# VectorE makes 7 tokens and one single product, ScalarE three products, in the second output tile of each group from the second on

## The chip, the cores and the metric

The kernel runs on one core of a Trainium2 chip. A core has engines with instruction streams of their own: PE (TensorE, matrix products), DVE (VectorE, elementwise work on whole tiles), ACT (ScalarE, elementwise work with one scalar for each partition), POOL (GpSimd) and SP (SyncE, which here only issues transfers). They work on SBUF, an on-chip memory of 128 partitions. Transfers between SBUF and the large HBM memory run on 16 DMA engines, which all queues share. A transfer is issued by an engine's queue and signals a semaphore when it has landed.

The metric is the time of one execution on the device in microseconds (us). The time before is a median of 240.11 us over 3 runs.

## The reference

Every token's row of 512 numbers is written twice, once times each of the token's two expert weights:

```python
batch, seq, hidden, n_experts = 16, 1024, 512, 8
k = 2
x_expanded = x[:, :, np.newaxis, :].repeat(k, axis=2)
weights = expert_weights[..., np.newaxis]
return (x_expanded * weights).astype(np.float32)
```

`x` has 16,384 tokens, all in float32. The indices of the experts are not used. The input is 33.6 MB, the output twice that.

## The kernel before

The tokens are cut into seven groups of 19, 19, 18, 18, 18, 18 and 18 tokens for each of the 128 partitions (`groups`, line 30). In a group every partition holds consecutive tokens, so its share of a group is one contiguous piece of HBM. A group is loaded into an `x_tile` (two buffers) and written in two output tiles, `o_tile` (three buffers), its two "halves": 10 and 9 tokens for the first two groups, 9 and 9 for the others. An output tile of 9 tokens has 9 x 2 x 512 numbers a partition, 36,864 bytes.

The weights come in first by two small transfers. PE transposes them twice so that `w_tile` has, for each partition, the two weights of each of its tokens as columns (`weights_columns`, `weights_out`). This is over after the first group.

The loop at line 161 runs over the groups, and inside it over the two halves. For a half, `products` (line 134) makes the output tile, and SP issues its transfer to HBM (line 170). After both halves, `load(i + 2)` (line 176) has ScalarE's queue issue the load of the group after next into the buffer that has just been used up (line 128). The first group's load is cut in two; groups 0 and 1 are loaded ahead of the loop.

`products` splits a half of `n` tokens between two engines. VectorE makes the first `m` tokens, both weights of each, in one `tensor_tensor` (line 136), in which `x_tile` is repeated for the two weights and `w_tile` over the 512 numbers. ScalarE makes the rest, one `mul` for each token and weight (line 149), each 512 numbers a partition with the weight as the scalar of the partition. `m` is all of the tokens in the very first half and `n - 1` afterwards, so that ScalarE has two products in each half but the first.

The order of instructions on each engine is the order in which the program is written (`manual_schedule`, line 110). Semaphores add the waits: a product waits for its `x_tile` to be loaded and for its `o_tile` to be free, that is, for the output transfer that last read it; a transfer of the output waits for both engines' products; a load waits until both engines have read the old group. On ScalarE's queue a load therefore stands between the products of one group and those of the next.

Of the kernel before, what the change touches and what calls it, by code (L numbers as in the profile page):

```python
# [1 line left out]

# [4 lines left out]


@with_exitstack
def kernel(  # L10
    ctx: ExitStack,
    tc: tile.TileContext,
    x: bass.AP,
    expert_indices: bass.AP,
    expert_weights: bass.AP,
    out: bass.AP,
):
    nc = tc.nc

    batch, seq, hidden = x.shape  # L20
    k = expert_weights.shape[-1]
    P = nc.NUM_PARTITIONS
    ntok = batch * seq
    assert ntok % P == 0

    f32 = mybir.dt.float32
    row = k * hidden


    groups = [19, 19, 18, 18, 18, 18, 18]  # L30
    assert sum(groups) * P == ntok
    TX = max(groups)
    TO = (TX + 1) // 2

    xf = x.rearrange("b s h -> (b s) h")
    of = out.rearrange("b s k h -> (b s) (k h)")
    wf = expert_weights.rearrange("b s k -> (b s) k")

    w_pool = ctx.enter_context(tc.tile_pool(name="w_pool", bufs=1))
    x_pool = ctx.enter_context(tc.tile_pool(name="x_pool", bufs=2))  # L40
    o_pool = ctx.enter_context(tc.tile_pool(name="o_pool", bufs=3))

    raw_pool = ctx.enter_context(tc.tile_pool(name="raw_pool", bufs=1))
    psum = ctx.enter_context(
        tc.tile_pool(name="psum", bufs=2, space=bass.MemoryType.PSUM)
    )

    w_tile = w_pool.tile([P, sum(groups) * k], f32)

    def rows(flat, done, T):  # L50
        return flat[done * P : (done + T) * P, :].rearrange("(p a) n -> p (a n)", a=T)

    B = 8
    M = P // B
    ident = w_pool.tile([P, P], f32)
    nc.gpsimd.memset(ident, 0.0)  # L59
    nc.gpsimd.affine_select(  # L60
        out=ident,
        in_=ident,
        compare_op=mybir.AluOpType.not_equal,
        fill=1.0,
        base=0,
        pattern=[[-1, P]],
        channel_multiplier=1,
    )

    def weights_in(eng, head, G, T):  # L70
        raw_tile = raw_pool.tile([G * M, B * T * k], f32, name=f"raw{T}_tile")
        eng.dma_start(
            out=raw_tile,
            in_=wf[head * P : (head + G * T) * P, :].rearrange(
                "(q a) n -> q (a n)", a=B * T
            ),
        )
        return raw_tile

    def weights_columns(raw_tile, G, T):  # L80
        n = T * k
        col_tile = raw_pool.tile([n, G * P], f32, name=f"col{T}_tile")
        cols = col_tile.rearrange("c (q r) -> c q r", r=B)
        for r0 in range(0, B, B // 2):
            up_tile = psum.tile([n, B // 2, G * M], f32)
            for r in range(B // 2):
                nc.tensor.transpose(  # L87
                    up_tile[:, r, :],
                    raw_tile[:, (r0 + r) * n : (r0 + r + 1) * n],
                    ident[: G * M, : G * M],  # L90
                )
            nc.vector.tensor_copy(  # L92
                out=cols[:, :, r0 : r0 + B // 2],
                in_=up_tile.rearrange("c r q -> c q r"),
            )
        down_tile = psum.tile([P, G * n], f32)
        for g in range(G):
            nc.tensor.transpose(  # L98
                down_tile[:, g * n : (g + 1) * n],
                col_tile[:, g * P : (g + 1) * P],  # L100
                ident[:n, :n],
            )
        return down_tile

    def weights_out(down_tile, head, G, T):
        nc.vector.tensor_copy(  # L106
            out=w_tile[:, head * k : (head + G * T) * k], in_=down_tile
        )

    ctx.enter_context(tc.manual_schedule())  # L110

    starts = [sum(groups[:i]) for i in range(len(groups))]
    loaded = []


    def halves(i):
        T = groups[i]
        return [T - T // 2, T // 2]

    def load(i):  # L120
        if i >= len(groups):
            return
        x_tile = x_pool.tile([P, TX * hidden], f32)
        loaded.append(x_tile)
        src = rows(xf, starts[i], groups[i])
        lo = 0
        for n in halves(i) if i == 0 else [groups[i]]:
            nc.scalar.dma_start(
                out=x_tile[:, lo * hidden : (lo + n) * hidden],
                in_=src[:, lo * hidden : (lo + n) * hidden],  # L130
            )
            lo += n

    def products(o_tile, x_tile, at, n, w_at):
        m = n - 1 if w_at else n
        nc.vector.tensor_tensor(  # L136
            out=o_tile[:, : m * row].rearrange("p (t k h) -> p t k h", t=m, k=k),
            in0=x_tile[:, at * hidden : (at + m) * hidden]
            .rearrange("p (t h) -> p t h", t=m)
            .unsqueeze(2)  # L140
            .to_broadcast([P, m, k, hidden]),
            in1=w_tile[:, w_at : w_at + m * k]
            .rearrange("p (t k) -> p t k", t=m)
            .unsqueeze(3)
            .to_broadcast([P, m, k, hidden]),
            op=mybir.AluOpType.mult,
        )
        for c in range(m * k, n * k):
            nc.scalar.mul(  # L149
                out=o_tile[:, c * hidden : (c + 1) * hidden],  # L150
                in_=x_tile[:, (at + c // k) * hidden : (at + c // k + 1) * hidden],
                mul=w_tile[:, w_at + c : w_at + c + 1],
            )

    raw_a = weights_in(nc.sync, starts[0], 2, 19)
    load(0)
    raw_b = weights_in(nc.scalar, starts[2], 5, 18)
    load(1)
    weights_out(weights_columns(raw_a, 2, 19), starts[0], 2, 19)

    for i, T in enumerate(groups):
        x_tile = loaded[i]
        outr = rows(of, starts[i], T)
        at = 0
        for j, n in enumerate(halves(i)):
            if i == 0 and j == 1:
                down_b = weights_columns(raw_b, 5, 18)
            o_tile = o_pool.tile([P, TO * row], f32)
            products(o_tile, x_tile, at, n, (starts[i] + at) * k)
            nc.sync.dma_start(  # L170
                out=outr[:, at * row : (at + n) * row], in_=o_tile[:, : n * row]
            )
            at += n
        if i == 0:
            weights_out(down_b, starts[2], 5, 18)
        load(i + 2)

# [1 line left out]
_INS = ['x', 'expert_indices', 'expert_weights']  # L179
_OUTS = [((16, 1024, 2, 512), 'float32')]  # L180


# [23 lines left out]
```

## Time and profile before

| what | value |
|---|---|
| median of 3 runs | 240.11 us (239.59 to 240.15) |
| the profiled execution | 240.3 us |
| its span (first to last instruction) | 238.3 us |
| granted clock | 1.00 |
| VectorE products (line 136) | 14, 124.9 us busy |
| ScalarE products (line 149) | 26, 17.3 us busy |
| output transfers (line 170) | 14: two of 5120 KB, twelve of 4608 KB |
| loads of x (line 128) | 8 |
| HBM read and written | 33.69 MB and 67.11 MB |

The page of a profile gives each engine's busy time as a share of the span. It then gives the DMA queues, with the time that their packets took as a share of what 16 engines have in the span, and the chain of work that ended last, followed back from the last instruction. Instructions are grouped by source line, with the tile written and the tiles read, and their size as partitions x elements. Behind the bar stand the busy time and the mean duration in ns, then the engine's idle time just before them and what ended it. A transfer is listed with its size and the time from its issue to its landing. Windows give the same figures for a chosen stretch of time; a DMA packet is counted in the window in which it begins, so a short window can show a share above 1.

### The profile page before, as it was taken

The numbers are of one execution on the slowest core, as the hardware profiler recorded it, in microseconds if no ns is written. First come the engines' busy times: TensorE is split into PE (matmuls) and PEld (weight loads), VectorE is DVE, ScalarE is ACT, GpSimd is POOL, SyncE is SP. The second block draws the span as 40 slices with busy tenths as digits, with TensorE's granted clock in tenths as the row PEclk, the third lists the DMA queues.
The fourth block names the chain that finished last, engine by engine and source line by source line (L and its number), as shares of the span: only waits on it lengthen the run. The fifth ranks groups of instructions, "written<-read, shape, count | busy, mean of one in ns | idle before, by whom it ended". The sixth has DMA issues, their size and how long they took to land.

```text
span 238.3 us, 213 instructions
## 1 busy us (share of the span) xinstructions
PE 3.0 (1%) x23; PEld 2.3 (1%) x23; DVE 126.6 (53%) x20; ACT 18.6 (8%) x27; POOL 0.7 (0%) x6
## 2 busy tenths in 40 slices
PE   1021000000000000000000000000000000000000
PEld 1011000000000000000000000000000000000000
DVE  1499987391095077950494900778504949680000
ACT  0040020200020020200202000202002020200000
POOL 1000000000000000000000000000000000000000
DMA  7999899999999999999999999999999999999995
GB/s 275 426 465 425 352 443 473 404 402 483 404 424 418 439 483 402 421 470 402 446 439 402 483 402 421 439 427 446 415 433 458 421 433 433 427 446 415 433 458 235
DMA packets 3312, 100.80 MB, mean 423 GB/s; under 512 B 384, under 2 KB 496, under 8 KB 496
## 3 DMA queue, kind: packets, MB, share of 16 engines
q1 hardware_dynamic: 2064, 67.15, 65.4%
q10 hardware_dynamic: 1248, 33.65, 33.3%
HBM read 33.69 MB, written 67.11 MB: 423 GB/s over the span
## 4 chain that ended last, share of the span: by engine, by line
DMA 66%; DVE 23%; issue 0%; DVEq 0%; SPq 0%
DMA out_dram<-o_tile 62%; DVE o_tile L136 23%; DMA x_tile<-in_x_dram 4%; DVE col_tile L92 0%; DVEq L136 0%; SPq L170 0%
## 5 line engine op out<-in xcount | busy, mean ns | idle before, releaser
L136 DVE TENSOR_TENSOR o_tile<-x_tile,w_tile 128x8192 f32<-128x8192 f32 (+2 forms) x14 | 124.9, 8920 | 82.5 <-DMA out_dram<-o_tile 77.6
L149 ACT ACTIVATE o_tile<-x_tile,w_tile 128x512 f32<-128x512 f32 x26 | 17.3, 714 | 172.4 <-DMA out_dram<-o_tile 159.6
L92 DVE COPY col_tile<-up_tile 38x128 f32<-38x128 f32 (+1 forms) x4 | 1.4, 378 | 4.0 <-PE up_tile L87 4.0
L149 ACT ACT_TABLE_LOAD x1 | 1.3, 1283 | 15.3 <-DMA x_tile<-in_x_dram 15.3
L87 PE MATMUL up_tile<-ident,raw_tile 32*38 32x32 f32 (+1 forms) x16 | 1.8, 284 | 14.3 <-DMA raw_tile<-in_expert_weights_dram 14.3
L87 PEld LDWEIGHTS up_tile<-ident,raw_tile 32*38 32x38 f32 (+1 forms) x16 | 1.4, 135 | 14.4 <-issue 14.4
L98 PE MATMUL down_tile<-ident,col_tile 36*128 36x36 f32 (+1 forms) x7 | 1.2, 305 | 4.7 <-DVE col_tile L92 4.7
L98 PEld LDWEIGHTS down_tile<-ident,col_tile 36*128 36x128 f32 (+1 forms) x7 | 0.9, 209 | 5.1 <-DVE col_tile L92 5.1
L106 DVE COPY w_tile<-down_tile 128x76 f32<-128x76 f32 (+1 forms) x2 | 0.6, 284 | 0.5 <-PE down_tile L98 0.5
L60 POOL TENSOR_SCALAR_AFFINE_SELECT ident<-ident 128x128 f32<-128x128 f32 x1 | 0.3, 292 | 0.1
L59 POOL MEMSET ident<- 128x128 f32 x1 | 0.2, 204 | 0.3 <-POOLq L190 0.3
L190 POOL MEMSET const-bfloat16-1.0<- 128x1 bf16 x1 | 0.1, 101 | 0.0
L190 POOL MEMSET const-uint8-127<- 128x1 uint8 x1 | 0.1, 101 | 0.0
L190 POOL MEMSET const-float32-0.0<- 128x1 f32 x1 | 0.1, 98 | 0.2 <-issue 0.2
L190 POOL MEMSET const-float32-1.0<- 128x1 f32 x1 | 0.1, 98 | 0.0
## 6 DMA issues: line engine op xcount, KB each, us to landing
out_dram<-o_tile SPq DMA_DIRECT2D x12, 4608.0 KB, 35.4
x_tile<-in_x_dram ACTq DMA_DIRECT2D x5, 4608.0 KB, 26.6
out_dram<-o_tile SPq DMA_DIRECT2D x2, 5120.0 KB, 34.8
x_tile<-in_x_dram ACTq DMA_DIRECT2D x1, 4864.0 KB, 27.5
x_tile<-in_x_dram ACTq DMA_DIRECT2D x1, 2560.0 KB, 8.7
x_tile<-in_x_dram ACTq DMA_DIRECT2D x1, 2304.0 KB, 14.0
raw_tile<-in_expert_weights_dram ACTq DMA_DIRECT2D x1, 90.0 KB, 13.9
raw_tile<-in_expert_weights_dram SPq DMA_DIRECT2D x1, 38.0 KB, 2.7
```

Of the source, the lines that this page charges most:

```text
L59: nc.gpsimd.memset(ident, 0.0)
L60: nc.gpsimd.affine_select(out=ident, in_=ident, compare_op=mybir.AluOpType.not_equal, fill=1.0, base=0, pattern=[[-1, P]], channel_multipl ...
L87: nc.tensor.transpose(up_tile[:, r, :], raw_tile[:, (r0 + r) * n : (r0 + r + 1) * n], ident[: G * M, : G * M],)
L92: nc.vector.tensor_copy(out=cols[:, :, r0 : r0 + B // 2], in_=up_tile.rearrange("c r q -> c q r"),)
L98: nc.tensor.transpose(down_tile[:, g * n : (g + 1) * n], col_tile[:, g * P : (g + 1) * P], ident[:n, :n],)
L106: nc.vector.tensor_copy(out=w_tile[:, head * k : (head + G * T) * k], in_=down_tile)
L136: nc.vector.tensor_tensor(out=o_tile[:, : m * row].rearrange("p (t k h) -> p t k h", t=m, k=k), in0=x_tile[:, at * hidden : (at + m) * hidden]
L149: nc.scalar.mul(out=o_tile[:, c * hidden : (c + 1) * hidden], in_=x_tile[:, (at + c // k) * hidden : (at + c // k + 1) * hidden], mul=w_ti ...
L190: nc = _bacc.Bacc("TRN2", target_bir_lowering=False, num_devices=1)
```

## The change

From the second group on, the second half of a group is split in another way. VectorE's large product covers 7 of the 9 tokens in place of 8. VectorE then makes one more product itself, of a single token and weight, as a `tensor_scalar` with the weight as scalar. ScalarE makes the remaining three of these single products in place of two. The first halves, and both halves of the first group, stay as they were. Six output tiles are concerned.

```diff
-    def products(o_tile, x_tile, at, n, w_at):
-        m = n - 1 if w_at else n
+
+    def products(o_tile, x_tile, at, n, w_at, m, s):
         nc.vector.tensor_tensor(
             out=o_tile[:, : m * row].rearrange("p (t k h) -> p t k h", t=m, k=k),
             in0=x_tile[:, at * hidden : (at + m) * hidden]
...
             op=mybir.AluOpType.mult,
         )
         for c in range(m * k, n * k):
-            nc.scalar.mul(
-                out=o_tile[:, c * hidden : (c + 1) * hidden],
-                in_=x_tile[:, (at + c // k) * hidden : (at + c // k + 1) * hidden],
-                mul=w_tile[:, w_at + c : w_at + c + 1],
-            )
+            out = o_tile[:, c * hidden : (c + 1) * hidden]
+            x_in = x_tile[:, (at + c // k) * hidden : (at + c // k + 1) * hidden]
+            w = w_tile[:, w_at + c : w_at + c + 1]
+            if c < m * k + s:
+                nc.vector.tensor_scalar(
+                    out=out, in0=x_in, scalar1=w, scalar2=None, op0=mybir.AluOpType.mult
+                )
+            else:
+                nc.scalar.mul(out=out, in_=x_in, mul=w)
...
             o_tile = o_pool.tile([P, TO * row], f32)
-            products(o_tile, x_tile, at, n, (starts[i] + at) * k)
+
+            m, s = (n - 2, 1) if i and j else (n - 1, 0) if i or j else (n, 0)
+            products(o_tile, x_tile, at, n, (starts[i] + at) * k, m, s)
```

## The prediction

> **What bounds the kernel now.** I read the page first: the shares of the engines, then the DMA queues, then the chain that ended last.
>
> ```profile
> span 238.3 us, 213 instructions
> PE 3.0 (1%) x23; PEld 2.3 (1%) x23; DVE 126.6 (53%) x20; ACT 18.6 (8%) x27; POOL 0.7 (0%) x6
> DMA packets 3312, 100.80 MB, mean 423 GB/s; under 512 B 384, under 2 KB 496, under 8 KB 496
> q1 hardware_dynamic: 2064, 67.15, 65.4%
> q10 hardware_dynamic: 1248, 33.65, 33.3%
> DMA 66%; DVE 23%; issue 0%; DVEq 0%; SPq 0%
> ```
>
> VectorE (DVE) is busy half of the time and ScalarE (ACT) a twelfth. The two DMA queues, q1 for the outputs and q10 for the loads, together take 65.4 + 33.3 = 98.7% of what 16 DMA engines have in the span. The last line, the chain, gives VectorE 23%, which invites the thought that a shorter product shortens the kernel. So the second view is the DMA by stretches of time. The columns are the stretch, its length, the busy time of PE, PEld, DVE, ACT and POOL, the clock, the DMA share and GB/s.
>
> ```profile
> 20.00:234.00 214.00, 0.75 (x5) 0.61 (x5) 115.38 (x17) 16.01 (x24) 0.00 (x0) 1.00 1.00 432
> 200.00:234.00 34.00, 0.00 (x0) 0.00 (x0) 11.43 (x2) 1.33 (x2) 0.00 (x0) 1.00 1.00 434
> 235.00:236.00 1.00, 0.00 (x0) 0.00 (x0) 0.00 (x0) 0.00 (x0) 0.00 (x0) 1.00 0.51 221
> 236.00:237.00 1.00, 0.00 (x0) 0.00 (x0) 0.00 (x0) 0.00 (x0) 0.00 (x0) 1.00 0.01 0
> ```
>
> From 20 to 234 us the share is 1.00 at 432 GB/s, and it stays 1.00 at 434 GB/s after 200 us, when only outputs are left. A share of 1.00 means that all 16 engines always have a packet. All 100.80 MB at 432 GB/s take 233.3 us; the other 5.0 us of the span are the start, before there is anything to move, and the end. The change moves not a byte more or less.
>
> The third view asks how long a finished tile waits in the queue: the transfers of the output, over the whole span (first fence) and from 195 us on (second).
>
> ```profile
> L170 SPq DMA_DIRECT2D out_dram<-o_tile x14: 332/332/357, 20.4 to 213.7; - x14
> DMA to landing us min/median/max: 23.8/35.4/45.8
> ```
>
> ```profile
> L170 SPq DMA_DIRECT2D out_dram<-o_tile x2: 332/332/332, 202.8 to 213.7; - x2
> out_dram<-o_tile SPq DMA_DIRECT2D x2, 4608.0 KB, 23.8
> DMA to landing us min/median/max: 23.8/23.8/23.8
> ```
>
> A tile of 9 tokens is 4608 KB = 4.72 MB, at 434 GB/s 10.9 us of all engines. Yet no output lands sooner than 23.8 us after its issue. The last two were issued at 202.8 and 213.7 and landed at 226.6 and 237.5: exactly one transfer apart. The last tile was therefore handed over 226.6 - 213.7 = 12.9 us before the engines finished the one ahead of it. A transfer that found nothing ahead of it would still need its start-up. The smallest one in the trace bounds that:
>
> ```profile
> raw_tile<-in_expert_weights_dram SPq DMA_DIRECT2D x1, 38.0 KB, 2.7
> ```
>
> So the last changed tile could be 12.9 - 2.7 = 10.2 us later before an engine ran dry. The end of the kernel is set by bytes through the engines, and VectorE has a **cover of 10.2 us** there.
>
> The six products that the change touches are the second of each pair from 45 us on:
>
> ```profile
> 45.60 8.69 DVE L136 TENSOR_TENSOR o_tile<-x_tile,w_tile 128x8192 f32<-128x8192 f32 x1 [5.24 <-DMA out_dram<-o_tile]
> 84.95 8.69 DVE L136 TENSOR_TENSOR o_tile<-x_tile,w_tile 128x8192 f32<-128x8192 f32 x1 [10.22 <-DMA out_dram<-o_tile]
> 116.23 8.69 DVE L136 TENSOR_TENSOR o_tile<-x_tile,w_tile 128x8192 f32<-128x8192 f32 x1 [11.71 <-DMA out_dram<-o_tile]
> 150.50 8.69 DVE L136 TENSOR_TENSOR o_tile<-x_tile,w_tile 128x8192 f32<-128x8192 f32 x1 [13.30 <-DMA out_dram<-o_tile]
> 181.77 8.69 DVE L136 TENSOR_TENSOR o_tile<-x_tile,w_tile 128x8192 f32<-128x8192 f32 x1 [11.62 <-DMA out_dram<-o_tile]
> 204.93 8.69 DVE L136 TENSOR_TENSOR o_tile<-x_tile,w_tile 128x8192 f32<-128x8192 f32 x1 [2.19 <-DMA out_dram<-o_tile]
> ```
>
> In each the bracket says that VectorE stood idle before it until an earlier output had left the buffer that the product writes. With three buffers, one has then just landed and two are still in the queue: up to two transfers of 10.9 us against a product of 8.7 us, which gives 13.1 us, close to the 12.9 read above. VectorE waits for the DMA and not the other way round.
>
> **The change part by part.** *VectorE.* The product has three sizes in the trace, and there is a copy of two sizes as well:
>
> ```profile
> L136 DVE TENSOR_TENSOR o_tile<-x_tile,w_tile 128x8192 f32<-128x8192 f32 x12 | 104.3, 8692 | 77.6 <-DMA out_dram<-o_tile 77.6
> L136 DVE TENSOR_TENSOR o_tile<-x_tile,w_tile 128x10240 f32<-128x10240 f32 x1 | 10.8, 10826 | 4.3 <-DMA x_tile<-in_x_dram 4.3
> L92 DVE COPY col_tile<-up_tile 36x320 f32<-36x320 f32 x2 | 0.9, 474 | 0.0
> L106 DVE COPY w_tile<-down_tile 128x180 f32<-128x180 f32 x1 | 0.3, 329 | 0.0
> ```
>
> (10826 - 8692) / 2048 = 1.042 ns an element, and 8692 - 8192 x 1.042 = 156 ns fixed. Seven tokens, 7168 elements, come to 7.63 us, which is 1.07 less. The single product of 512 elements by one scalar a partition has no row. Nothing in the trace streams faster than 1.04 ns an element; for a lower bound I halve that, 156 + 512 x 0.52 = 0.42 us. Its upper bound is a second fixed part and two cycles an element, 156 x 2 + 512 x 2.08 = 1.38 us. The nearest rows are the copies, also with one input tensor: (474 - 329) / 140 = 1.04 ns an element, so 474 + 192 x 1.04 = 0.67 us. I take 0.67. A changed tile then needs 7.63 + 0.67 = 8.30 us against 8.69, so it is handed over 0.39 us earlier; by the bounds, 0.64 earlier to 0.32 later.
>
> The Trainium skill ("VectorE: DVE Perf Modes", The perf-mode tier table) lets an fp32 product with a scalar run at 2x from SBUF, while an fp32 product of two tensors stays at 1x. By that rule the estimate is the lower bound, about 0.43 us, and 0.63 us earlier; no row here has such an operation, and the time of the kernel would be the same.
>
> *ScalarE.* It gets a third product of this kind:
>
> ```profile
> L149 ACT ACTIVATE o_tile<-x_tile,w_tile 128x512 f32<-128x512 f32 x26 | 17.3, 714 | 172.4 <-DMA out_dram<-o_tile 159.6 <-DMA x_tile<-in_x_dram 12.7
> 204.92 1.33 ACT L149 ACTIVATE o_tile<-x_tile,w_tile 128x512 f32<-128x512 f32 x2 [9.57 <-DMA out_dram<-o_tile]
> ```
>
> 17.3 / 26 = 0.67 us each, so three take 2.0 us in place of 1.33. They start with VectorE's (204.92 beside 204.93) and end 6.3 us before its 8.30 are over, so they cost nothing; if ScalarE ran after VectorE and not beside it, the tile would be 8.30 + 2.0 = 10.3 us, 1.6 later than now and still inside the 10.2 of cover.
>
> *What is queued behind.* The load of the group after next is issued by ScalarE's queue once both engines have finished the second tile; the output is issued by SP's. Both move with the tile, 0.39 us earlier, and neither queue gets a DMA more.
>
> ```profile
> 124.99 0.33 SPq L170 DMA_DIRECT2D out_dram<-o_tile  x1
> 125.02 0.36 ACTq L128 DMA_DIRECT2D x_tile<-in_x_dram  x1
> DVE o_tile L136 <- DMA out_dram<-o_tile: 77.6, 11, 13.3
> DVE o_tile L136 <- DMA x_tile<-in_x_dram: 4.9, 2, 4.3
> ```
>
> VectorE waits for a load only twice, 4.9 us in all, 4.3 of it before the very first product (10240 elements); an earlier load is hidden. The 0.39 us go into the wait for a buffer, which is 77.6 us in 11 waits: VectorE idles that much longer, and each finished tile lies that much longer in the queue.
>
> *Sum.* The profiled execution took 240.3 us, with a span of 238.3. VectorE -6 x 0.39 = -2.3 us, all of it off the path; ScalarE +6 x 0.67 = +4.0 us, off the path; DMA bytes 0; path 0. That leaves 240.3. The median of the runs is 240.11, 0.19 below the profiled one, and I set the forecast on it: **240.1 us**.
>
> What can still move is the end. In the last two windows the engines do not stop together: 221 GB/s is 0.22 MB, six packets of 36,864 bytes (one partition's 9 tokens), begun after 235 us, while the other ten engines begin none. One packet on one engine takes 36,864 B / (432 / 16 GB/s) = 1.37 us. How the engines end up staggered may shift by half a packet either way, 0.7 us. That and the spread of the runs, 239.59 to 240.15, make the forecast's own range 239.4 to 240.8.
>
> **The rivals.** *Faster, by the chain taken at its word.* Two of the VectorE products in the chain belong to changed tiles:
>
> ```profile
> 116.23 8.71 DVE o_tile L136
> 124.99 36.28 DMA out_dram<-o_tile
> 204.93 8.69 DVE o_tile L136
> ```
>
> If each link shortened the end, 2 x 0.39 = 0.8 us would be gained, 2 x 0.64 = 1.3 by the lower bound: 239.3 down to 238.8 us on the median. Against it stands the link between them: a transfer worth 10.9 us of all engines takes 36.28 from issue to landing, so the chain runs through a queue that has other work to do, and that queue never empties (share 1.00).
>
> *Slower, because the single product stops the transfers.* The new operation may read SBUF at double rate through both ports and hold up the DMA engines that read the output tiles there. The place is the six single products; the price is at most their whole time, 6 x 0.67 = 4.0 us, or 6 x 0.42 = 2.5: 242.6 to 244.1 us. It decides from 0.72 / 6 = 0.12 us of stand-still at each. For it speaks only that no such operation is in the trace. Against it: with VectorE busy for 115.38 of 214 us the share is 1.00, and between products it is no better:
>
> ```profile
> 204.90:213.60 8.70, 0.00 (x0) 0.00 (x0) 8.67 (x1) 1.33 (x2) 0.00 (x0) 1.00 0.97 419
> 213.70:234.00 20.30, 0.00 (x0) 0.00 (x0) 0.00 (x0) 0.00 (x0) 0.00 (x0) 1.00 0.99 429
> ```
>
> 419 against 429 GB/s is a few packets counted on one side of an edge. The Trainium skill ("SBUF — State Buffer", Who interferes with whom) says that a VectorE operation in a two-port mode shuts out GpSimd, and so only the DMAs whose descriptors GpSimd writes. By that rule these transfers, of the kind hardware_dynamic on both queues, lose nothing and this rival falls; no run here shows it yet.
>
> *Slower, because a changed tile comes too late* (the pair of VectorE instructions costs far more than its rows, or a wait between the engines is added). Its price is only what exceeds the 10.2 us of cover, at the last tile; even the serial order above costs 1.6 of it. *That the change does not do what it says*, the product still of eight tokens, gives the same 240.1.
>
> **How the numbers follow.** A measurement of this kernel tells about 0.3%, 0.72 us, from no change. No change, with the range 239.4 to 240.8: 0.88. The chain at its word, 0.04, and a gain at the staggered end, 0.01, make faster 0.05. Stopped transfers 0.05 and a late tile or something unseen 0.02 make slower 0.07. The forecast's own range already leaves only 0.12 outside, so it stays the range.
>
> **What would show it.** Right: products of 7168 elements of 7.6 us, six single products of 0.4 to 0.7 us on VectorE, 32 ScalarE products in place of 26, VectorE's wait for output buffers longer by about 2 us than 77.6, the share still 1.00 at 432 GB/s from 20 to 234 us, the last two outputs still landing 10.9 us apart. The cover is wrong if the DMA share of any long stretch falls below 1.00, or if the shortest time to landing falls towards 10.9 us. The chain reading is right if the last output lands about 0.8 us sooner after the start although the GB/s stay the same; the port reading is right if the GB/s dip at the six single products.

## The result and the profile after

| | before | after |
|---|---|---|
| median of 15 runs | 239.68 us | 241.56 us |
| lowest and highest | 239.41, 242.02 | 239.52, 242.72 |
| runs above 240.6 us | 2 of 15 | 12 of 15 |
| the profiled execution | 240.3 us | 239.52 us |
| its span | 238.3 us | 237.6 us |

The changed kernel is **slower**: the ratio of the times is 1.0058, 95% interval 1.003 to 1.0085, against a forecast of no change. Both kernels reach 239.5 us, but the changed one seldom does; most of its executions take 241 to 242.7. The profiled execution happened to be the fastest of its 15, so this profile can't show the loss by itself. A later profile of the same kernel, its third, is of an execution of 241.25 us, and the two are shown side by side. In this document the ratios leave out executions more than 1.5% above the fastest of the same kernel (five in all), while medians, ranges and counts are over all executions.

First the page of the profiled execution, in the lines that answer to those of before:

```profile
span 237.6 us, 225 instructions
PE 3.0 (1%) x23; PEld 2.3 (1%) x23; DVE 122.6 (52%) x26; ACT 22.3 (9%) x33; POOL 0.7 (0%) x6
q1 hardware_dynamic: 2064, 67.15, 65.6%
q10 hardware_dynamic: 1248, 33.65, 33.3%
```

VectorE has 4.0 us less to do and ScalarE 3.7 more; the queues carry the same bytes. The groups of instructions, shapes kept apart, and the wait of VectorE for output buffers, in the same execution:

```profile
L136 DVE TENSOR_TENSOR o_tile<-x_tile,w_tile 128x7168 f32<-128x7168 f32 x6 | 45.7, 7625 | 54.9 <-DMA out_dram<-o_tile 54.9
L157 ACT ACTIVATE o_tile<-x_tile,w_tile 128x512 f32<-128x512 f32 x32 | 21.0, 713 | 168.6 <-DMA out_dram<-o_tile 155.9 <-DMA x_tile<-in_x_dram 12.6
L153 DVE TENSOR_SCALAR o_tile<-x_tile,w_tile 128x512 f32<-128x512 f32 x6 | 2.9, 480 | 0.0
```

```profile
DVE o_tile L136 <- DMA out_dram<-o_tile: 80.3, 11, 13.0
```

The reader sees the split as it was meant: a product of 7168 elements in 7.63 us, a single product in 0.48, and a wait for buffers that has grown from 77.6 to 80.3 us. One changed tile in order of time:

```profile
115.60 1.95 ACT L157 ACTIVATE o_tile<-x_tile,w_tile 128x512 f32<-128x512 f32 x3 [18.96 <-DMA out_dram<-o_tile]
115.69 7.62 DVE L136 TENSOR_TENSOR o_tile<-x_tile,w_tile 128x7168 f32<-128x7168 f32 x1 [11.66 <-DMA out_dram<-o_tile]
123.24 0.48 DVE L153 TENSOR_SCALAR o_tile<-x_tile,w_tile 128x512 f32<-128x512 f32 x1
123.78 0.33 SPq L176 DMA_DIRECT2D out_dram<-o_tile  x1
123.80 0.36 ACTq L128 DMA_DIRECT2D x_tile<-in_x_dram  x1
```

From the start of VectorE's product to the issue of the output it is 123.78 - 115.69 = 8.09 us; before it was 124.99 - 116.23 = 8.76. The tile is handed over 0.67 us earlier. I call this time, start of the product to issue of the output, the **hand-over time** below.

Now the end of the kernel. The windows have the columns of the prediction's; first the profiled execution, then the third profile, of 241.25 us:

```profile
20.00:234.00 214.00, 0.75 (x5) 0.61 (x5) 111.35 (x23) 19.69 (x30) 0.00 (x0) 1.00 1.00 433
235.00:236.00 1.00, 0.00 (x0) 0.00 (x0) 0.00 (x0) 0.00 (x0) 0.00 (x0) 1.00 0.09 37
236.00:237.00 1.00, 0.00 (x0) 0.00 (x0) 0.00 (x0) 0.00 (x0) 0.00 (x0) 1.00 0.01 0
```

```profile
20.00:234.00 214.00, 0.74 (x5) 0.60 (x5) 111.44 (x23) 19.69 (x30) 0.00 (x0) 1.00 1.00 432
235.00:236.00 1.00, 0.00 (x0) 0.00 (x0) 0.00 (x0) 0.00 (x0) 0.00 (x0) 1.00 0.34 147
236.00:237.00 1.00, 0.00 (x0) 0.00 (x0) 0.00 (x0) 0.00 (x0) 0.00 (x0) 1.00 0.26 111
```

From 20 to 234 us the two executions, 1.73 us apart in time, show the same share and 433 against 432 GB/s. The difference stands in the last row. One packet of 36,864 bytes begun in a window of 1 us counts 37 GB/s. In the first table a single packet begins after 235 us and none after 236; in the second, three packets (111 GB/s) begin after 236. They are the last packets of three DMA engines that run 1.8 us behind the other thirteen.

The trace has every DMA packet with its queue, start, duration and size, though not its engine. On a busy engine a packet begins 3 or 4 ns before the one ahead of it ends, so the packets string together into 16 sequences, one for each engine. This assignment is an inference, and after a pause on an engine it rests on which packet no other sequence explains. From them come the ends of the last output tile on the engines (us from the first instruction):

| profile | time | median engine ends | last engine ends | time - last end |
|---|---|---|---|---|
| before | 240.3 | 236.24 | 237.13 | 3.2 |
| before, second profile | 240.46 | 236.25 | 237.30 | 3.2 |
| after | 239.52 | 236.11 | 236.38 | 3.1 |
| after, second profile | 241.03 | 236.23 | 238.00 | 3.0 |
| after, third profile | 241.25 | 236.17 | 237.99 | 3.3 |

The median engine ends within 0.14 us of the same moment in all five. The time follows the last engine. Here is one of the thirteen engines and one of the late three in the third profile of after (start of the packet in us; o output, L load, s the small packet that signals the end of a transfer; the duration in ns where it isn't 1364; in brackets idle ns between packets):

```
on time  159.79:s  159.80:o  161.16:o        162.52:L        163.88:o        165.24:L        166.60:o
late     160.79:s  160.80:o  162.16:o 1929   (218) 164.30:L 1491  165.79:o   167.15:L
```

Both have packets of two queues to alternate between from 162 us on, when the load issued at 158.69 arrives. The late engine, 1.0 us behind at this point, takes 1929 ns for an output packet in place of 1364, then stands still for 218 ns and takes 1491 ns for its first load packet, and falls 0.91 us further behind. The other two late engines do much the same here. All three had lost about 0.4 us each before that, on the last packets of an earlier load (115.5 to 115.7 us: 1736 to 1766 ns), and nothing to speak of anywhere else after the start. In the other execution, of 241.03 us, two engines lost 1.5 and 1.1 us in the same two places, at 115.4 and 162.0 to 164.5 us.

### The profile page after: what moved, and what is told of

The parts are those of the page before. It is cut to its first block, busy times and chain, and to the rows that moved or that the text cites. A ratio compares the mean times of both kernels' runs of the same rounds, so it can differ in the third digit from the quotient of the medians.

```text
span 237.6 us, 225 instructions
## 1 busy us (share of the span) xinstructions
PE 3.0 (1%) x23; PEld 2.3 (1%) x23; DVE 122.6 (52%) x26; ACT 22.3 (9%) x33; POOL 0.7 (0%) x6
## 4 chain that ended last, share of the span: by engine, by line
DMA 66%; DVE 21%; issue 2%; DVEq 0%; SPq 0%
DMA out_dram<-o_tile 62%; DVE o_tile L136 20%; DMA x_tile<-in_x_dram 4%; DVE col_tile L92 0%; DVE o_tile L153 0%; DVEq L207 0%; DVEq L136 0%; SPq L176 0%
## 5 line engine op out<-in xcount | busy, mean ns | idle before, releaser
L136 DVE TENSOR_TENSOR o_tile<-x_tile,w_tile 128x8192 f32<-128x8192 f32 (+3 forms) x14 | 118.5, 8462 | 85.2 <-DMA out_dram<-o_tile 80.3
L157 ACT ACTIVATE o_tile<-x_tile,w_tile 128x512 f32<-128x512 f32 x32 | 21.0, 713 | 168.6 <-DMA out_dram<-o_tile 155.9
L153 DVE TENSOR_SCALAR o_tile<-x_tile,w_tile 128x512 f32<-128x512 f32 x6 | 2.9, 480 | 0.0
```

The costliest lines, as they stand in the source:

```text
L136: nc.vector.tensor_tensor(out=o_tile[:, : m * row].rearrange("p (t k h) -> p t k h", t=m, k=k), in0=x_tile[:, at * hidden : (at + m) * hidden]
L153: nc.vector.tensor_scalar(out=out, in0=x_in, scalar1=w, scalar2=None, op0=mybir.AluOpType.mult)
L157: nc.scalar.mul(out=out, in_=x_in, mul=w)
```

## The experiments

The runs have 10 to 15 timed executions, those without the loop's loads 4 and 5, and two runs were made for a profile alone. Each ratio is to the kernel before, timed in the same session on the same chip. The four kernels under "The remainder" were on a second chip and the two without loads on a third; the experiments ahead of them, with the changed kernel again, were all on one. The summary table stands at the end of this section.

**The changed kernel again**, no edit.

> The changed kernel as it is. Theory P (the split in itself moves the end): about 241.5 us, 1.8 above the kernel before, and a profile of one such execution shows where. Theory N (the measured difference is scatter from execution to execution that both kernels have): both medians within 0.7 us of each other, 239.5 to 240.5.

241.04 us against 240.04 for the kernel before in the same session, ratio 1.0023 (1.000 to 1.0046); 8 of 12 runs above 240.6 against 5 of 35. The loss is there again, about half as large (1.0 us in the medians against 1.9). Its profile (241.03 us) shows two late engines, the fourth row of the table above. Theory N falls, the place is a few engines.

**Undo parts of the split.** Three edits of the one line that sets it, and one that leaves the split and adds instructions:

```diff
-            m, s = (n - 2, 1) if i and j else (n - 1, 0) if i or j else (n, 0)
+            m, s = (n - 2, 0) if i and j else (n - 1, 0) if i or j else (n, 0)
```

> VectorE 7 tokens, ScalarE four products, no single product on VectorE; a changed tile is handed over 1.07 us earlier than before (0.6 in the changed kernel). Theory H (the earlier hand-over costs): 241.5 us or more. Theory S (the single product on VectorE itself costs): 239.7 as before. Theory C (more instructions cost): the count is the changed kernel's, with 12 more on ScalarE and none on VectorE, so about 241.5.

239.88 us, ratio to before 0.9986 (0.9964 to 1.0007), 1 of 12 above 240.6. The tile is handed over even earlier (7.69 us), and nothing is lost. Theory H falls as it stood, and so does the count of instructions on ScalarE: it has 12 more than before.

```diff
-            m, s = (n - 2, 1) if i and j else (n - 1, 0) if i or j else (n, 0)
+            m, s = (n - 1, 1) if i and j else (n - 1, 0) if i or j else (n, 0)
```

> VectorE 8 tokens and one single product, ScalarE one product; a changed tile is handed over about 0.5 us later than before. Theory H (the earlier hand-over costs): 239.7 us or less. Theory S (the single product on VectorE costs): 241.5. Theory C (more instructions cost): six more on VectorE, six fewer on ScalarE, so 239.7 if it is the sum, 241.5 if it is VectorE's own count.

239.79 us, ratio 0.9986 (0.9967 to 1.0005), 1 of 12 above 240.6. It has the same six single products on VectorE as the changed kernel, as its groups show:

```profile
L153 DVE TENSOR_SCALAR o_tile<-x_tile,w_tile 128x512 f32<-128x512 f32 x6 | 2.9, 481 | 0.0
```

So the operation that is new in the changed kernel costs the kernel nothing by itself (theory S falls).

```diff
             products(o_tile, x_tile, at, n, (starts[i] + at) * k)
+            if i and j:
+                nc.vector.tensor_tensor(
+                    out=pad_v, in0=w_tile[:, 0:2], in1=w_tile[:, 2:4], op=mybir.AluOpType.mult
+                )
+                nc.scalar.mul(out=pad_s, in_=w_tile[:, 0:2], mul=w_tile[:, 2:3])
```

> The split of before, and in each of the six tiles one product of 2 numbers a partition more on VectorE and one on ScalarE, on a tile of their own that nothing waits for. Theory C (more instructions cost): 241.5 us. Theories H and S (hand-over, single product): 239.7 as before.

240.46 us, ratio 1.0016 (0.9986 to 1.0046), 5 of 12 above 240.6: between the two, and not told apart from before. Inconclusive; the number of instructions alone speaks neither for nor against.

**One queue for loads and outputs.** If the engines lose their time where a second queue begins or ends, one queue should spare them:

```diff
-    def load(i):
+    def load(i, eng):
...
-            nc.scalar.dma_start(
+            eng.dma_start(
...
-    load(0)
+    load(0, nc.scalar)
...
-    load(1)
+    load(1, nc.scalar)
...
-        load(i + 2)
+        load(i + 2, nc.sync)
```

> The changed kernel with the five loads of the loop issued on SP's queue, behind the group's second output, in place of ScalarE's; the loads ahead of the loop stay. Theory Q (the extra time is single DMA engines that stop for up to 1 us where the loads' queue begins or ends beside the outputs' queue; the split only moves these moments): with one queue left after the start, 239.0 to 239.7 us, no run above 240.5, and the last tile's engines end within 0.7 us of each other. Theory P (the split itself costs, whatever the queues): about 241, 1 us above the same queue arrangement with the split of before. Theory L (a load behind two outputs comes too late): slower than 243 for both.

> The kernel before with the same single queue for the loop's loads. Theory Q: 239.0 to 239.7 us, the same as the changed split on one queue within 0.3 us, and less scatter than on two queues. Theory P: 239.7 to 240.0, 1 us below the changed split on one queue.

242.47 us with the changed split (ratio to before 1.0074, 1.0043 to 1.0106) and 242.55 with the split of before (1.0094, 1.0064 to 1.0124). Theory Q missed on the time: one queue is slower for both, and every run is above 240.6. Theory L's mark of 243 was not reached either. It was right in one point, that the two splits are then the same, within 0.1 us. The windows at the end of the first show what the time consists of:

```profile
235.00:236.00 1.00, 0.00 (x0) 0.00 (x0) 0.00 (x0) 0.00 (x0) 0.00 (x0) 1.00 0.34 147
236.00:237.00 1.00, 0.00 (x0) 0.00 (x0) 0.00 (x0) 0.00 (x0) 0.00 (x0) 1.00 0.18 74
238.00:239.00 1.00, 0.00 (x0) 0.00 (x0) 0.00 (x0) 0.00 (x0) 0.00 (x0) 1.00 0.09 37
```

One packet begins as late as 238 us: a single engine ends at 239.69, 3.4 us behind the median one at 236.24. Its long packets begin at 60.2, 94.4, 126.8, 158.8 and 191.8 us; these are the moments when the last packets of a load give way to outputs. No second queue is needed for a loss, then, but a load next to outputs is there in every case so far.

**All six singles on VectorE**, and a third profile of the changed kernel:

```diff
-            m, s = (n - 2, 1) if i and j else (n - 1, 0) if i or j else (n, 0)
+            m, s = (n - 1, 2) if i and j else (n - 1, 0) if i or j else (n, 0)
```

> Two queues as before; in the six tiles VectorE makes 8 tokens and two single products, ScalarE none, so the hand-over comes about 0.8 us later than before, which is the changed kernel's 0.6 us earlier plus one packet time of 1.37. Theory F (what counts is where the hand-over falls in the rhythm of the packets): as slow as the changed kernel, 241 us. Theory V (an earlier hand-over costs, a later one does not): 239.7. Theory S (the single product on VectorE costs): 241.5 or more.

241.22 us, ratio 1.0032 (0.9998 to 1.0066), 8 of 12 above 240.6 (the kernel before: 3 of 25); hand-over time 9.51 us. Here a later hand-over looks as bad as the changed kernel's earlier one, as theory F had it, though the interval just reaches 1. The end of its profile (242.36 us) is of another kind, however:

```profile
235.00:236.00 1.00, 0.00 (x0) 0.00 (x0) 0.00 (x0) 0.00 (x0) 0.00 (x0) 1.00 1.28 553
236.00:237.00 1.00, 0.00 (x0) 0.00 (x0) 0.00 (x0) 0.00 (x0) 0.00 (x0) 1.00 0.18 74
237.00:238.00 1.00, 0.00 (x0) 0.00 (x0) 0.00 (x0) 0.00 (x0) 0.00 (x0) 1.00 0.09 37
238.00:239.00 1.00, 0.00 (x0) 0.00 (x0) 0.00 (x0) 0.00 (x0) 0.00 (x0) 1.00 0.09 37
```

553 GB/s are 15 packets begun after 235 us, against six in the kernel before. The median engine ends at 236.76, 0.5 us later than in the five profiles above, and the last at 239.40. All 16 engines had load packets of 1500 to 2151 ns between 112 and 115.5 us. That is not at the edge of the load, whose packets run from 98.9 to 119.9 us, but next to the end of an output transfer.

> The changed kernel once more for a second look at a slow execution. Theory Q: if its span is above 239 us, the DMA engines end their last packets 1.5 us or more apart, and the late ones have lost their time at the begin or end of a load, while the middle engines end at the same time as in the kernel before. Theory P: all engines end late together.

241.25 us: the third profile of the section on the result. Theory Q's picture of the end (late engines, the others on time) is what it shows.

**Shift the load alone**, on both splits (shown on the split of before; on the changed one the slice read is the single product's):

```diff
+        if i:
+            end = (n - 1) * row
+            nc.scalar.mul(
+                out=pad_s, in_=o_tile[:, end - hidden : end], mul=w_tile[:, 0:1]
+            )
         load(i + 2)
```

> The kernel before, with one more ScalarE product of 512 numbers into a tile of its own behind each group's second tile (from the second group on); it reads what VectorE made last, so only the group's load is issued later, by about 0.75 us, and the outputs are not. Theory F-load (what decides is where the load's issue falls against the packets that the engines are in): as slow as the kernel with all six singles on VectorE, whose hand-over is 0.8 us later, about 241 us, with late engines that lost 0.5 to 1 us where a load begins. Theory F-out (the output's hand-over decides): 239.9 as before.

> The changed kernel with the same extra ScalarE product ahead of the load: outputs handed over 0.6 us earlier than before, the load issued 0.1 us later than before. Theory F-load: 239.9, as the kernel before. Theory F-out: 241.2, as the changed kernel.

239.63 us (ratio 0.9991, 0.997 to 1.0012; 1 of 12 above 240.6) and 241.25 us (1.003, 1.0004 to 1.0056; 9 of 12). Read against the expectations this would be theory F-out. But the edit did not do what it was to do, as the timeline of the first one shows:

```profile
158.52 0.33 SPq L171 DMA_DIRECT2D out_dram<-o_tile  x1
158.55 0.72 ACT L179 ACTIVATE pad_s<-o_tile,w_tile 128x512 f32<-128x512 f32 x1 [7.55 <-DVE o_tile L137]
158.58 0.35 ACTq L129 DMA_DIRECT2D x_tile<-in_x_dram  x1
```

The load is issued 0.03 us after the extra product begins, and does not wait for its 0.72 us. The load still leaves with the output (0.06 us later in place of 0.03), so nothing is told about load against output. What the pair gives is a repetition of both splits with an instruction more on ScalarE, and the same gap between them: 1.6 us in the medians. The profile of the second (241.34 us) shows two engines that end at 238.2 and 238.3 us, with most of their loss at the places of the changed kernel's other two long profiles, 115.6 to 115.9 and 162.3 to 164.2 us.

**Two tokens' worth further.** The same line with `(n - 3, 0)`:

> VectorE 6 tokens, ScalarE six products in the six tiles: outputs and load 2.1 us earlier than before, that is 1.4 us (one packet) earlier than in the changed kernel. Theory F (the place in the rhythm of 1.37 us packets decides): about 241 us. Theory W (only small shifts disturb; a tile that is 1.07 us earlier was as fast as before): 239.9.

241.03 us, ratio 1.0052 (1.0029 to 1.0074), 11 of 12 above 240.6; hand-over time 6.62 us. Theory W falls, and the loss is there though VectorE makes no single product at all. Its two late engines (last end 237.92, median 236.23) lost their time at 127.6 to 129.5 us, in the first packets of another load.

> The kernel before once more, for the scatter of its DMA engines: at a span of about 238 us the last tile's engines end within 1.2 us; if the span is above 239, late engines again, with their losses where a load begins or ends.

240.46 us: one late engine, at 237.30, which had lost 0.5 us more than the others at the start of the kernel (25.6 us) and 0.4 at 114.4 us. The kernel before has the same ailment, less of it.

**The remainder.** By now the slower kernels had hand-over times of 6.62, 8.09 and 9.51 us and the others 7.69, 8.76 and 9.15, which separate by what remains after whole packet times of 1.36 us. Four kernels test this; the first and the last are the same line with `(n - 2, 3)` and `(n - 2, 2)`, the middle ones have `(n - 1, 2)` and repeat the last single:

```diff
+            for _ in range(2 if s == 2 and c == n * k - 1 else 0):
+                nc.vector.tensor_scalar(
+                    out=out, in0=x_in, scalar1=w, scalar2=None, op0=mybir.AluOpType.mult
+                )
```

> VectorE 7 tokens and three single products, ScalarE one. From the start of VectorE's product to the issue of the output the traces so far give 6.62, 8.09 and 9.51 us for the slower kernels and 7.69, 8.76 and 9.15 for those that are not; the remainders after whole packet times of 1.36 us are 1.18, 1.29, 1.35 and 0.89, 0.60, 0.99. This one should take about 8.87, remainder 0.71. Theory F (the remainder decides): 239.9, as before. Theory S (each single product on VectorE costs): 242 or more, above the changed kernel.

> VectorE 8 tokens and two single products, the second one made three times over, ScalarE none: about 10.27 us from the product's start to the issue, remainder 0.75. Theory F: 239.9, as before, although it is 0.76 us later than the kernel with 9.51 us that had 241.2. Theory V (a later hand-over costs from some point on): 241.5 or more. Theory S: 243.

> The same with the second single made four times and once more for its first 128 numbers: about 10.84 us, remainder 1.32. Theory F: slow again, 241.0 to 241.5. If it is as fast as before, theory F falls.

> VectorE 7 tokens and two single products, ScalarE two: about 8.48 us, remainder 0.32, which no kernel so far has. Theory F leaves it open: 239.9 if the slow remainders end by 1.36, 241 if they reach past it. Theory S: about 241.5, between the changed kernel and three singles.

Three singles: 240.69 us (1.0028, 1.0001 to 1.0055; 7 of 12 above 240.6, where the kernel before had 4 of 35) at a hand-over time of 8.88, remainder 0.72: above 240.6, where theory F had it below. Repeated singles: 241.23 (1.0023, 0.9984 to 1.0061; 7 of 12) at 10.56, remainder 1.04, and 240.92 (1.0027, 0.9994 to 1.006; 8 of 12) at 11.40, remainder 0.52. Both came out longer than meant, so their remainders are not the ones they were built for; the second nevertheless lies between 0.32 and 0.60, the remainders of two kernels below 240.6, and is above it. Its profile (241.70 us) shows the other kind of loss again: all 16 engines had load packets of 1.6 to 2.1 us at 111 to 112.6 us and of 1.9 to 2.6 us at 177 to 178.2 us, again in the middle of a load, and the median engine ends at 237.81. Two singles: 239.90 (1.0006, 0.9978 to 1.0033; 3 of 12) at 8.48. **Theory F falls**: the remainder sorted six kernels and failed on the next, whose interval only just clears 1. Theory S is out: with 7 tokens on VectorE and none, one, two or three singles the medians are 239.88, 241.0 to 241.6, 239.90 and 240.69, and on the first chip alone the kernel of 6 tokens without a single is slower while that of 8 tokens with one is not.

**Without the loop's loads**, on both splits:

```diff
-        x_tile = loaded[i]
+        x_tile = loaded[i % 2]
...
-        load(i + 2)
```

> The changed kernel without the five loads of the loop: groups 2 to 6 multiply the tokens of groups 0 and 1 again. 23.6 MB less at 432 GB/s, 54.6 us less: 185.5 us. Theory Q (the losses need a load that begins or ends beside outputs): the same as the split of before without these loads, within 0.3 us, hardly any scatter (all runs within 1 us), and no DMA engine loses time after the start. Theory P (the split itself costs): 1 us above it.

> The kernel before without the five loads of the loop. 185.5 us; by theory Q the same as the changed split without loads within 0.3 us, by theory P 1 us below it.

185.57 us (185.49 to 185.83, four runs) with the changed split and 185.43 (185.15 to 185.78, five) with that of before: the same within 0.14 us, and hardly any scatter. The bytes and the share of the second of them:

```profile
HBM read 10.09 MB, written 67.11 MB: 420 GB/s over the span
20.00:180.00 160.00, 0.74 (x5) 0.61 (x5) 115.30 (x17) 16.01 (x24) 0.00 (x0) 1.00 1.00 431
```

The queue is as full as before, 431 GB/s at a share of 1.00. After 30 us not one packet in either trace is over 100 ns longer than 1364 ns. Theory Q holds in this form: **the engines lose time after the start only while there are loads beside outputs, and without these loads the change shows no difference** (0.14 us between medians of four and five executions, whose ranges overlap).

The split kernels together, by hand-over time (the line of before has all six sessions):

| VectorE, ScalarE in the six tiles | hand-over us | median us | ratio to before (95%) | above 240.6 |
|---|---|---|---|---|
| 6 tokens; 6 singles | 6.62 | 241.03 | 1.0052 (1.0029 to 1.0074) | 11 of 12 |
| 7 tokens; 4 singles | 7.69 | 239.88 | 0.9986 (0.9964 to 1.0007) | 1 of 12 |
| 7 + 1 single; 3 (the change) | 8.09 | 241.56, 241.04 | 1.0058 (1.003 to 1.0085), 1.0023 (1.000 to 1.0046) | 20 of 27 |
| 7 + 2; 2 | 8.48 | 239.90 | 1.0006 (0.9978 to 1.0033) | 3 of 12 |
| 8 tokens; 2 (before) | 8.76 | 239.68 to 240.18 | 1 | 19 of 147 |
| 7 + 3; 1 | 8.88 | 240.69 | 1.0028 (1.0001 to 1.0055) | 7 of 12 |
| 8 + 1; 1 | 9.15 | 239.79 | 0.9986 (0.9967 to 1.0005) | 1 of 12 |
| 8 + 2; 0 | 9.51 | 241.22 | 1.0032 (0.9998 to 1.0066) | 8 of 12 |
| 8 + 4 (one repeated); 0 | 10.56 | 241.23 | 1.0023 (0.9984 to 1.0061) | 7 of 12 |
| 8 + 5 and a short one (one repeated); 0 | 11.40 | 240.92 | 1.0027 (0.9994 to 1.006) | 8 of 12 |

No version beats the kernel before beyond its interval.

## Why the prediction was wrong

**VectorE's and ScalarE's terms were right in kind.** The product of 7168 elements was forecast at 7.63 us and took 7.62 to 7.63. The single product was forecast at 0.67 and took 0.48, close to the lower bound of 0.42. The row of the copies, which read PSUM tiles, was a poor neighbour; the estimate from the Trainium skill ("VectorE: DVE Perf Modes", The perf-mode tier table), 0.43 us at the 2x rate, was nearer, and the 0.48 us of the trace agree with that rule better than with a 1x rate (156 + 512 x 1.042 = 690 ns). The single also begins 0.08 us before the product ends, so the tile came 0.67 us earlier, not 0.39, just past my bound of 0.64. Three ScalarE products took 1.95 us, forecast 2.0, beside VectorE's.

**The cover was right.** VectorE's wait for buffers grew by 2.7 us (forecast about 2), the share from 20 to 234 us stayed 1.00 at 433 GB/s, and no queue ran dry. Seven tokens and four singles move the hand-over by another 0.4 us at no cost.

**The step that failed** is the one from the share to the end: "A share of 1.00 means that all 16 engines always have a packet", and from there "path 0" in the sum. The share is the time that packets took. A packet that takes 1929 ns for 1364 ns of work counts as busy, and one engine of sixteen that loses 1 us in a window of 214 is 0.03% of it. The end is set not by that mean but by the slowest engine. I saw the stagger, gave it 0.7 us, and took it to be independent of the change. It is neither: the last engine ended 0.9 to 1.05 us behind the median in the two profiles of before, 0.27 in the profile of after shown above, and 1.8 in its two others. That term, put at nothing in the change's account, grew by 0.7 to 0.9 us and accounts for the 0.6 to 0.95 us between these longer profiles and those of before to within 0.2 us: the median engine ends at the same time. The medians of the two sessions differ by more, 1.9 and 1.0 us, and no profile shows such a pair of executions. That the same term makes up the rest is inferred: in all 18 profiles of kernels with the loop's loads the time is 3.0 to 3.5 us after the last engine's end.

**The rivals.** The chain at its word is refuted: with an earlier hand-over of 0.67 us the time did not fall, and with 1.07 us (7 tokens and 4 singles) it did not either. The single product as a brake on the transfers is refuted by the kernel with 8 tokens and one single, which has as many of them and is not slower; in the third profile the long packets lie at 115.5 and 162 to 164 us, while the nearest single products are at 123.7 and 158.1. No tile came too late. The chance of 0.07 for slower named two mechanisms, and the right one was neither of them; it can only have been in the "something unseen".

**What stays open.** Shown is where the changed kernel's time goes (two or three engines, mostly at the first and last packets of a load), that losses need the loads, and that the time depends on the split. What differs is less the amount lost than how few engines lose it. Packets over 100 ns too long, with the pauses, add up after 30 us to 3.4 us on seven engines in the profile of before (at most 0.66 on one), and to 2.9 us on eleven with 7 tokens and four singles (at most 0.44). In the second and third profile of the changed kernel they add up to 2.6 us on two engines and 3.7 us on three, 1.1 to 1.5 us on each. Not shown is how the split decides which engine is caught. It is not the number of singles, nor earlier or later as such, nor the hand-over's place in the packet rhythm alone. The load and the output of a tile are issued within 0.03 us of each other in all of these kernels, and the one attempt to part them failed, so which of the two matters is open. That engines already behind are the ones caught fits the two traces of the changed kernel that took longer (in the third profile the three were 0.7 to 0.84 us behind the first engine from 44 us on). The profile of before speaks against it as a rule: there the engine that was 0.96 us behind at 44 us lost only 0.16 us in a long packet afterwards, while five engines that were 0.2 to 0.5 us behind lost 0.5 to 0.66 us each at 148 us. No run set an engine's lag on purpose. Nor is it shown why in two profiles (8 tokens and two singles at 242.36 us, the last kernel with repeated singles at 241.70 us) all engines had long packets at once.

## What to carry to other kernels

A DMA share of 1.00 said here that nothing is gained by handing work over sooner; it did not say that the engines finish together. Where transfers bound a kernel, look at the last microseconds packet by packet, and time a dozen executions before reading one profile, since the one that was profiled may be the best of them. A change far off the path of a transfer-bound kernel can still move its time by half a per cent while loads run beside outputs; through which moment it did so here is open.

## What the runs showed of the hardware

DMA engines lose up to about 1 us at a time while a load runs beside outputs. In the changed kernel's longer profiles it was two or three of 16 engines, mostly at the first or last packets of a load, with up to 2046 ns for packets of 1364 ns, while the others went on undisturbed. In two other kernels' profiles it was all 16, in the middle of a load, with up to 2151 and 2566 ns. Without loads in the loop no packet after 30 us took over 100 ns longer than 1364. Loads on the outputs' own queue made it worse, 242.5 us for both splits. And a load that ScalarE's queue issues does not wait for the product ahead of it: it was issued 0.03 us into a product of 0.72 us.
